# One layer of a conformer trunk on one core: the head's load order, unread matmuls in the stands, shares between VectorE and GpSimd, and a joint last group

## The chip, the cores and the metric

The kernel runs on one core of a Trainium2 chip. The metric is device time in microseconds (us), the median of several executions; lower is better. TensorE (PE) multiplies, with a weight load (PEld) ahead of each matmul; VectorE (DVE), ScalarE (ACT) and GpSimd (POOL) do the elementwise work; SyncE (SP) issues the DMAs.

## What is computed

All in fp32, for 1024 tokens of width D = 1024. With `DEPTH = 1` only the first mixer, the convolution module, is run, and only the latent tokens:

```python
mod_l = (silu(c) @ w_mod + b_mod)                       # 6 vectors of 1024
sh1, s1, g1, sh2, s2, g2 = split(mod_l, 6)
h = rms_norm(x, norm1_g) * (1 + s1) + sh1
u = h @ w_pw1 + b_pw1;  a, gate = split(u, 2)
u = dwconv(a * sigmoid(gate), w_dw) + b_dw              # 31 taps, inside segments of 64 tokens
u = silu(layer_norm(u, ln_g, ln_b))
x = x + g1 * (u @ w_pw2 + b_pw2)
h = rms_norm(x, norm2_g) * (1 + s2) + sh2
x = x + g2 * (square(relu(h @ w1)) @ w2)                # hidden width 4096
return rms_norm(x, final_g)
```

## The kernel before

Channels lie on the 128 partitions in 8 chunks, tokens on the free axis, in two blocks of 512: A (b = 0) and B (b = 1). Each fp32 operand of a product is split into a high and a low part (`fp32r`): ACT casts the high part, DVE or POOL subtracts it for the low one (`split_lo`, `weights`, `first_weights`, `split_wide`; all of these subtractions have line L373). A product is three matmuls of 512 columns (L424 to L426, in the second half of the MLP L890 to L892).

The stages, in order:

- **Head** (L1008 to L1028). Loads by SP: the conditioning vector `craw` first, then block A's 8 tiles of x, then the modulation rows and first weights, chunk by chunk. ACT squares x (L488), DVE sums the squares, PE makes the mean in a "turned" form (tokens on partitions, L451), ACT the root (L506), DVE its reciprocal, PE spreads it again (L521), ACT copies it (L526). `mod_chunk` makes 128 entries of one modulation vector from 512 KB of `w_mod`: on DVE in one instruction (L568) or on POOL (L576) with two instructions on ACT behind it (L581, L584). `modulated` (L534, L549, L553) makes the operand, and PE runs 8 accumulations of 24 matmuls.
- **Conv A beside the first pointwise product of B.** PE does ten pairs of `PW1_ORDER`, 48 matmuls each. Of the 31 taps of a chunk three start the sums, `POOL_TAPS` go to POOL (L703, after a multiply on ACT, L698), `PE_TAPS` to PE as diagonal matrices in plain fp32 (L668), and the others to DVE (L713). L723 and L732 add the sums up.
- **Layer norm A** (`layer_norm`: L747 subtracts the mean, L488 squares, L446 feeds the mean on PE, L499 root, L501 reciprocal, L759 multiplies, L764 silu).
- **Second pointwise product A** (`pointwise2`, 8 outputs of 24 matmuls; L779 adds to x), with the rows of `G1`, `S2`, `SH2` made chunk by chunk; then `norm2` A, with the two pairs of `PW1_LATE` behind it on PE.
- **First MLP product of A** (`up_first`, 32 outputs n of 24 matmuls, results to DRAM), beside conv B, whose chunk c has the turn `CONV_B[c]` = 3c in units of n. At n = `LN_B` = `PW2_B` = 22 come layer norm B, the second pointwise product B and `norm2` B.
- **8 groups of the second MLP product.** Seven groups (`mlp_joint`) do both blocks with seven instead of eight block products, at the price of eight sums and differences (`plus`, engines `S_ENG`, `T_ENG`) and of splits of the seven pairs (`WLO_ENG`, `HLO_ENG`); a wave is one product of 24 matmuls. Between the first waves PE does four outputs of B's first product for the next group. After wave `GATE` the next group's loads may start. The last group (`mlp_apart`) does four waves for A, then four for B, and `finish` norms and stores each block.

Every instruction's place is set by hand-written planning at build time (`Plan`): each operation has an engine, a cost and a turn, and at each moment an engine takes the ready operation of the lowest turn, if it has a buffer (`SLOTS`, `CAPS`; an operation over `NEAR` turns ahead must leave `KEEP` buffers free). `SYNC` is the delay that the plan assumes between engines. A POOL instruction and a DVE instruction that reads SBUF alone (`port`) are planned one after the other, never together. The result is a fixed order on each engine and on SP's queue; each engine runs in order and waits on semaphores.

## Time and profile before

| | us |
|---|---|
| median of 3 runs | 1033.12 (1032.26 to 1034.19) |
| the profiled execution, time | 1034.25 |
| its span in the trace | 1032.4 |

| engine | busy, share of the span |
|---|---|
| PE matmul | 95% |
| PE weight load | 76% |
| DVE | 67% |
| POOL | 58% |
| ACT | 51% |

TensorE's granted clock is 0.986 of full speed in the mean. The 16 DMA engines move 125 MB, 121 GB/s over the span; only the first 55 us are filled by transfers (362 and 404 GB/s in the first two of 40 slices). A busy PE is not PE at its peak, since the ends of pipelined matmuls are modelled; the count of matmuls in a stretch says more. The chain that ended last goes almost all over PE's matmuls of the MLP.

### The profile page before, as it was taken

Reading aid. Unit: us, or ns where it says so; the run is one execution under the profiler, and the core shown is the slowest. Engines: PE = TensorE matmul, PEld = TensorE weight load, DVE = VectorE, ACT = ScalarE, POOL = GpSimd, SP = SyncE. Lnnn points to the kernel's source line nnn. Section 1 sums busy time; section 2 is a strip of 40 time slices with the busy share of each in tenths; the row PEclk is TensorE's granted clock in tenths of the full one; section 3 lists DMA queues with packets and bytes.
Section 4 is the critical chain, followed back from the end, with each engine's and each line's share of the span. In section 5 each row is a group of like instructions: output and inputs, shape, how many; then the busy total and the mean of one; then the engine's idle time right before and its main releaser. Section 6 shows DMA issues by size and latency. Waiting matters only on the chain. (4 is left out here: it accounts for less than half of the span.)

```text
span 1032.4 us, 11676 instructions
## 1 busy us (share of the span) xinstructions
PE 977.8 (95%) x4182; PEld 786.8 (76%) x4182; DVE 687.4 (67%) x941; ACT 524.0 (51%) x767; POOL 597.9 (58%) x366
## 2 busy tenths in 40 slices
PE   2999999959899999999999999999999999999994
PEld 1877767638688888788887888888788788878873
DVE  6979999996399991523265475665658565575453
ACT  5469566795667775763264434243252424342123
POOL 0049799989948999661347346437263462732324
PEclk9999999989999999999999999999999999999996
DMA  9920223445446444554151501504023040303012
GB/s 362 404 79 1 82 82 135 172 163 184 160 123 219 139 146 153 176 173 161 41 204 41 183 21 45 180 1 168 37 73 131 21 163 21 123 1 123 1 63 101
DMA packets 52522, 125.27 MB, mean 121 GB/s; under 512 B 4464, under 2 KB 21104, under 8 KB 52464
## 3 DMA queue, kind: packets, MB, share of 16 engines
q1 hardware_dynamic: 52464, 124.53, 34.3%
q8 instruction: 33, 0.54, 0.2%
q14 instruction: 25, 0.20, 0.1%
HBM read 111.93 MB, written 12.58 MB: 121 GB/s over the span
## 5 line engine op out<-in xcount | busy, mean ns | idle before, releaser
L373 POOL TENSOR_TENSOR big<-big 128x1024 fp32r<-128x1024 f32 (+1 forms) x144 | 351.0, 2454 | 303.3 <-DVE big L373 139.6
L424 PE MATMUL bank<-big 128*128 128x512 f32 x896 | 355.1, 396 | 10.8 <-ACT big L366 8.6
L426 PE MATMUL bank<-big 128*128 128x512 f32 x896 | 351.1, 392 | 1.7 <-POOL small L628 1.2
L425 PE MATMUL bank<-big 128*128 128x512 f32 x896 | 351.1, 392 | 0.8 <-DVE big L373 0.5
L779 DVE SCALAR_TENSOR_TENSOR small<-bank,mod,small 128x512 f32<-128x512 f32 x228 | 167.4, 747 | 215.3 <-PE bank L892 171.9
L424 PEld LDWEIGHTS bank<-big 128*128 128x128 f32 x896 | 169.5, 189 | 50.6 <-ACT big L366 9.4
L713 DVE SCALAR_TENSOR_TENSOR bank<-small,vec,bank 128x432 f32<-128x432 f32 (+10 forms) x323 | 200.9, 694 | 2.4 <-ACT bank L650 1.5
L425 PEld LDWEIGHTS bank<-big 128*128 128x128 f32 x896 | 169.3, 189 | 40.2 <-issue 2.1
L426 PEld LDWEIGHTS bank<-big 128*128 128x128 f32 x896 | 169.2, 189 | 37.9 <-POOL small L628 1.9
L891 PE MATMUL bank<-big 128*128 128x512 f32 x456 | 178.1, 391 | 3.4 <-POOL big L373 3.4
L890 PE MATMUL bank<-big 128*128 128x512 f32 x456 | 178.0, 390 | 0.0
L373 DVE TENSOR_TENSOR big<-big 128x1024 fp32r<-128x1024 f32 (+2 forms) x126 | 159.5, 1285 | 27.4 <-ACT big L386 12.5
L892 PE MATMUL bank<-big 128*128 128x512 f32 x456 | 177.5, 389 | 0.0
L850 ACT CAST big<-big 128x1024 fp32r<-128x1024 f32 x106 | 108.1, 1048 | 121.4 <-POOL big L373 52.8
L703 POOL TENSOR_TENSOR small<-small 128x392 f32<-128x392 f32 (+4 forms) x108 | 113.5, 1084 | 13.9 <-ACT small L698 9.7
L373 POOL TENSOR_TENSOR small<-small 128x512 f32<-128x512 f32 x46 | 59.7, 1301 | 93.6 <-ACT small L488 64.9
L386 ACT CAST big<-big 128x1024 fp32r<-128x1024 f32 x92 | 95.1, 1040 | 25.6 <-POOL big L373 25.2
L891 PEld LDWEIGHTS bank<-big 128*128 128x128 f32 x456 | 85.6, 188 | 23.6 <-POOL big L373 5.7
L890 PEld LDWEIGHTS bank<-big 128*128 128x128 f32 x456 | 85.6, 188 | 18.5 <-DVE small L976 0.4
L892 PEld LDWEIGHTS bank<-big 128*128 128x128 f32 x456 | 85.6, 188 | 17.6
L488 ACT ACTIVATE small<-small 128x512 f32<-128x512 f32 x64 | 38.4, 627 | 81.3 <-DVE small L779 78.3
L838 ACT ACTIVATE small<-bank 128x512 f32<-128x512 f32 x32 | 19.2, 599 | 110.0 <-PE bank L426 110.0
(65 smaller groups left out, 627.6 us busy)
## 6 DMA issues: line engine op xcount, KB each, us to landing
big<-in_w SPq DMA_DIRECT2D x96, 512.0 KB, 3.8
big<-in_wmod SPq DMA_DIRECT2D x48, 512.0 KB, 5.3
big<-in_wpw SPq DMA_DIRECT2D x28, 512.0 KB, 4.6
hidden<-small SPq DMA_DIRECT2D x32, 256.0 KB, 2.4
big<-hidden SPq DMA_DIRECT2D x16, 512.0 KB, 5.9
small<-in_xA SPq DMA_DIRECT2D x16, 256.0 KB, 4.1
big<-in_wfirst SPq DMA_DIRECT2D x8, 512.0 KB, 10.2
small<-in_xB SPq DMA_DIRECT2D x16, 256.0 KB, 6.0
```

What stands on the lines that cost most here:

```text
L373: lambda: eng_of[o.eng].tensor_tensor(out=out(), in0=a(), in1=b(), op=op), r, w, part=part, port=port,
L386: plan.op("act", c_act(D), lambda: act.copy(t(wh), t(raw)), [raw], [wh], also=[wl])
L424: pe.matmul(o, wh, hi(a)[:, s], start=first, stop=False)
L425: pe.matmul(o, wh, lo(a)[:, s], start=False, stop=False)
L426: pe.matmul(o, wl, hi(a)[:, s], start=False, stop=last)
L703: return pool.tensor_tensor(out=dst, in0=dst, in1=seg(t(m))[:, :, tt], op=ALU.add)
L713: dve.scalar_tensor_tensor(out=dst, in0=src, scalar=w, in1=dst, op0=ALU.mult, op1=ALU.add)
L779: lambda s=s, p=p: dve.scalar_tensor_tensor(out=t(x)[:, s], in0=cut(s, p), scalar=scale.t, in1=t(x)[:, s], op0=ALU.mult, op1=ALU.add,),
L850: plan.op("act", c_act(D), lambda: act.copy(t(h), t(x)), [x], [h], also=[l])
L890: pe.matmul(t(p), t(wh)[:, cs], t(hh)[:, ns], start=first and k == 0, stop=False, skip_group_check=not first)
L891: pe.matmul(t(p), t(wh)[:, cs], t(hl)[:, ns], start=False, stop=False, skip_group_check=not first)
L892: pe.matmul(t(p), t(wl)[:, cs], t(hh)[:, ns], start=False, stop=k == 1, skip_group_check=not first)
```

## The change

- Head: block A's x is loaded ahead of `craw`; the load of the sqrt table hangs on the last square instead of on `csil`; the first chunk reads the reciprocal root from PSUM, not from ACT's copy.
- `warm`: 8, 4, 6 and 11 matmuls of 128 columns on constants, whose result nothing reads: behind x's fourth tile, the head's root, the head's reciprocal root and layer norm A's reciprocal root.
- Of the 24 modulation chunks for `G1`, `S2` and `SH2`, all on POOL before, 12 go to DVE (3, 1 and 8). The loads of `G2` wait for conv A and then one for each output of `up_first`.
- The 32 low parts of `up_first`'s weights go from POOL to DVE (`UP_LO`).
- Taps: on PE 25 to 28 for A and 0 to 2 for B, on POOL 46 to 47 for A and 62 as before for B. `PW1_ORDER` has another order; `LN_B` and `PW2_B` go from 22 to 21.
- Groups: two of the four sums on POOL instead of one, other engines for the splits (POOL's number stays 7 of 14), `GATE` 3 to 2.
- The last group is joint: seven waves, no outputs of B's first product between them; A's outputs are complete at the fifth wave, B's at the seventh. Its sums of squares: A all added on DVE with one feed, B five added on POOL and three fed directly. Both blocks' last root is not turned; 3 of 8 last multiplies of each block go to POOL (before: of B alone).
- Layer norm B feeds its last two squares directly; `norm2` B's root is not turned.
- The plan's own numbers: `SYNC` by engine, other costs, `KEEP`, `NEAR`, `CAPS`. These may move any instruction.

```diff
-POOL_TAPS = ((5, 8, 5, 10, 5, 4, 7, 2), (10, 7, 5, 7, 8, 7, 9, 9))
+POOL_TAPS = ((7, 8, 6, 9, 5, 5, 4, 3), (10, 9, 8, 7, 10, 6, 7, 5))
-    (0, 4), (0, 5), (1, 0), (1, 1), (0, 6),
-    (0, 7), (1, 4), (1, 5), (1, 6), (1, 7),
+    (0, 4), (0, 5), (1, 0), (1, 4), (1, 5),
+    (0, 6), (0, 7), (1, 6), (1, 7), (1, 1),
-LN_B, PW2_B = 22, 22
-PE_TAPS = ((4, 2, 4, 4, 2, 2, 2, 5), (0, 0, 0, 0, 0, 0, 0, 0))
+LN_B, PW2_B = 21, 21
+PE_TAPS = ((2, 6, 2, 2, 2, 2, 5, 7), (0, 0, 2, 0, 0, 0, 0, 0))
-UP_LO = ("pool", "pool")
-S_ENG, T_ENG = ("dve", "dve", "pool", "dve"), ("dve", "dve", "dve", "dve")
-GATE = 3
-WLO_ENG, HLO_ENG = ("pool", "pool", "dve", "pool", "dve", "dve", "pool"), ("dve", "pool", "dve", "pool", "dve", "pool", "dve")
+UP_LO = ("dve", "pool")
+S_ENG, T_ENG = ("pool", "pool", "dve", "dve"), ("dve", "dve", "dve", "dve")
+GATE = 2
+WLO_ENG, HLO_ENG = ("dve", "pool", "dve", "dve", "dve", "pool", "pool"), ("dve", "pool", "dve", "dve", "pool", "pool", "pool")
-HEAD_DIRECT, LNA, LNB, N2B, FA = 0, 8, 0, 0, 1
-TURNED = (True, False, False, False, True, True)
+HEAD_DIRECT, LNA, LNB, N2B, FA = 0, 8, 2, 0, 0
+TURNED = (True, False, False, False, False, False)
-FIN_POOL = 3
-S2_ENG, G1_ENG = ("pool",) * 8, ("pool",) * 8
+WARM = (8, 4, 6, 11)
+LAST_JOINT = True
+FA_ENG, FB, FB_ENG = "dve", 3, "pool"
+FIN_POOL = (3, 3)
+S2_ENG, G1_ENG = ("pool", "pool", "dve", "pool", "pool", "pool", "pool", "pool"), ("pool", "pool", "pool", "dve", "dve", "pool", "dve", "pool")
+SH2_ENG, G2_ENG = ("dve", "dve", "dve", "dve", "dve", "dve", "dve", "dve"), "dve"
-KEEP = {"big": 2, "small": 3}
-NEAR = 2.0
-CAPS = {"raw": 4, "head": 7, "w": 8, "tmp": 6, "tap": 4, "taps": 4, "acc": 8, "wave": 14}
+KEEP = {"big": 4, "small": 2}
+NEAR = 120.0
+CAPS = {"raw": 4, "head": 7, "w": 10, "tmp": 4, "tap": 3, "taps": 4, "acc": 8, "wave": 12}
-    SYNC = 70
+    SYNC = {"pe": 200, "act": 140, "dve": 130, "pool": 80, "dma": 70}
...
+    def warm(n, after):
+        if not n:
+            return
+        p = new("bank", [P, BANK])
+        def emit():
+            for i in range(n):
+                pe.matmul(t(p)[:, :P], ones.t, ones.t, start=True, stop=True)
+        plan.op("pe", n * 220, emit, [ones, after], [p])
...
+        if b == 0:
+            warm(WARM[3], rstd)
...
-        run(s1, t1, q, True, (1, 1))
-        run(s4, b22, q, False, (1, 0))
-        run(a12, b21, r, True, (0, 0))
+        if g + 1 < NQ:
+            run(s1, t1, q, True, (1, 1))
+            run(s4, b22, q, False, (1, 0))
+            run(a12, b21, r, True, (0, 0))
+        else:
+            close(0, 1)
+            run(a12, b21, r, True, (0, 0))
+            close(0, 0)
+            run(s1, t1, q, True, (1, 1))
+            close(1, 1)
+            run(s4, b22, q, False, (1, 0))
+            close(1, 0)
+            finish(0, xls[0], sums[0])
+            finish(1, xls[1], sums[1])
...
+    xs0 = load_x(0)
     craw = new("big", [P, D], F32, "raw")
     plan.op("dma", 1460, lambda: sp.dma_start(t(craw), cvec.partition_broadcast(P)), w=[craw], lag=2000)
-    xs0 = load_x(0)
...
+    warm(WARM[0], xs0[3])
     for k in range(KC):
-        add_square(ms, xs0[k])
+        sq = add_square(ms, xs0[k])
     plan.op("act", c_act(D), lambda: act.activation(csil.t, t(craw), AF.Silu), [craw], [csil], "silu")
-    preload(AF.Sqrt, "sqrt", csil)
-    r0 = rstd_of(ms, False)
+    preload(AF.Sqrt, "sqrt", sq)
+    r0, r0_bank = rstd_of(ms, False, WARM[1])
+    warm(WARM[2], r0)
...
-        mod_chunk(S2, j, S2_ENG[j])
-        mod_chunk(SH2, j, S2_ENG[j])
+        mod_chunk(S2, j, S2_ENG[j], gate=conv_end(S2_GATE, j))
+        mod_chunk(SH2, j, SH2_ENG[j], gate=conv_end(S2_GATE, j))
...
-            mod_chunk(G2, n)
+            mod_chunk(G2, n, G2_ENG, gate=[up_op] if n else conv_end(7, 0))
...
-    sums = Mean(0, FA), Mean(1, 1, turned=TURNED[5])
+    sums = Mean(0, FA, FA_ENG), Mean(1, FB, FB_ENG, turned=TURNED[5])
...
-        if g + 1 < NQ:
-            mlp_joint(g, 2200 + 100 * g, lambda n: n < 5 and up_part(g + 1, n - 1))
+        if g + 1 < NQ or LAST_JOINT:
+            mlp_joint(g, 2200 + 100 * g, lambda n: n < 5 and g + 1 < NQ and up_part(g + 1, n - 1))
```

## Rows read from the trace of the kernel before

**Rows 1.** The page, parts 1 and 2: busy times; PE in 40 slices

```profile
PE 977.8 (95%) x4182; PEld 786.8 (76%) x4182; DVE 687.4 (67%) x941; ACT 524.0 (51%) x767; POOL 597.9 (58%) x366
PE   2999999959899999999999999999999999999994
```

**Rows 2.** Windows: length, busy PE PEld DVE ACT POOL (instructions), clock, DMA, GB/s

```profile
20.00:30.00 10.00, 7.83 (x25) 5.97 (x26) 9.64 (x17) 4.28 (x8) 0.00 (x0) 1.00 1.03 410
...
250.00:260.00 10.00, 10.00 (x46) 8.29 (x45) 1.62 (x4) 4.88 (x9) 10.00 (x7) 1.00 0.46 157
...
270.00:280.00 10.00, 7.23 (x21) 4.81 (x21) 3.77 (x3) 6.92 (x10) 10.00 (x5) 0.83 0.50 159
280.00:300.00 20.00, 20.00 (x89) 16.55 (x89) 18.52 (x28) 12.93 (x18) 10.93 (x8) 1.00 0.42 131
300.00:400.00 100.00, 100.00 (x443) 82.80 (x442) 86.68 (x141) 72.95 (x114) 92.40 (x66) 1.00 0.47 159
```

**Rows 3.** Timeline of the head: start, us, instruction [idle before <-releaser]

```profile
7.15 1.28 ACT L994 ACT_TABLE_LOAD   x1
...
8.45 0.29 ACT L994 ACTIVATE sc<-csil,eps 128x1 f32<-128x1 f32 x1
...
9.29 4.68 DVE L373 TENSOR_TENSOR small<-small 128x512 f32<-128x512 f32 x6 [1.44 <-ACT small L488]
...
13.89 1.28 DVE L568 CUSTOM_DVE_ANT_0 big<-big,csil,vec 128x1024 f32<-128x1024 f32 x1
...
17.59 2.04 PE L521 MATMUL bank<-small,ones 128*128 128x512 f32 x2 [1.70 <-DVE small L512]
...
21.85 0.80 PE L424 MATMUL bank<-big 128*128 128x512 f32 x1 [2.22 <-ACT big L549]
```

**Rows 4.** Timeline of layer norm A

```profile
217.17 3.35 DVE L501 RECIPROCAL bank<-bank 128x512 f32<-128x512 f32 x1
...
220.24 1.04 ACT L581 ACTIVATE big<-big 128x1024 f32<-128x1024 f32 x1
...
221.39 1.28 ACT L764 ACT_TABLE_LOAD   x1
...
224.21 0.79 PE L424 MATMUL bank<-big 128*128 128x512 f32 x1 [8.57 <-ACT big L366]
```

**Rows 5.** Timelines of DVE and ACT at the second norm of A

```profile
270.78 0.75 DVE L779 SCALAR_TENSOR_TENSOR small<-bank,mod,small 128x512 f32<-128x512 f32 x1 [0.37 <-PE bank L426]
...
272.26 1.06 ACT L581 ACTIVATE big<-big 128x1024 f32<-128x1024 f32 x1 [2.08 <-POOL big L576]
...
273.64 0.61 ACT L488 ACTIVATE small<-small 128x512 f32<-128x512 f32 x1
```

**Rows 6.** Groups by form: instructions, count | busy us, mean ns | idle before

```profile
L373 DVE TENSOR_TENSOR big<-big 128x1024 fp32r<-128x1024 f32 x61 | 81.0, 1333 | 15.1 <-ACT big L386 12.5 <-ACT big L850 1.6 <-issue 0.6
...
L713 DVE SCALAR_TENSOR_TENSOR bank<-small,vec,bank 128x448 f32<-128x448 f32 x32 | 20.7, 683 | 0.1
...
L373 POOL TENSOR_TENSOR big<-big 128x1024 fp32r<-128x1024 f32 x137 | 333.5, 2450 | 294.1 <-DVE big L373 130.4 <-DVE small L373 61.6 <-ACT big L850 48.6
...
L446 PE MATMUL bank<-small,ones 128*128 128x512 f32 x38 | 18.0, 603 | 7.1 <-ACT small L488 4.6 <-ACT small L612 1.7 <-POOL small L373 0.8
...
L668 PE MATMUL bank<-small,diag 128*128 128x408 f32 x12 | 5.0, 513 | 0.2 <-ACT diag L661 0.2
```

**Rows 7.** Waits of DVE from 290 to 430: waiter <- awaited, us, times, longest

```profile
DVE small L732 <- POOL small L703: 19.8, 4, 12.3
```

**Rows 8.** Waits of PE over the whole span

```profile
PE bank L891 <- POOL big L373: 3.4, 4, 1.6
```

**Rows 9.** Timelines of PE and POOL at the end

```profile
1012.92 0.39 PE L892 MATMUL bank<-big 128*128 128x512 f32 x1
1016.33 3.54 PE L451 MATMUL bank<-ones,small 128*128 128x1 f32 x16 [3.02 <-POOL small L373]
...
1023.99 3.71 POOL L373 TENSOR_TENSOR small<-small 128x512 f32<-128x512 f32 x3 [7.72 <-ACT small L968]
```

More of the change, by code (lines that the diff above doesn't have):

```diff
@@ L215, in run @@
                         a.left -= 1
-                        a.ready = max(a.ready, o.end + (0 if a.eng == o.eng else self.SYNC))
+                        a.ready = max(a.ready, o.end + (0 if a.eng == o.eng else self.SYNC[o.eng]))
                         if not a.left:
@@ L305, in c_pool, with load @@
     def c_pool(n):
-        return 80 + 2.15 * n
+        return 150 + 2.14 * n
     def c_tt(eng, n):
         return {"dve": c_dve(n), "pool": c_pool(n), "any": {"dve": c_dve(n), "pool": c_pool(n)}}[eng]
-    def load(buf, src, n, after=()):
+    def load(buf, src, n, after=(), gate=()):
         plan.op(
-            "dma", n * P * 4 / 360, lambda: sp.dma_start(t(buf)[:, :n], src), after, [buf], lag=2000
+            "dma", n * P * 4 / 360, lambda: sp.dma_start(t(buf)[:, :n], src), after, [buf], lag=2000,
+            gate=gate,
         )
@@ L456, in feed @@
             if self.turned:
-                plan.op("pe", 350 * QT, emit_turned, [x, ones], banks(self.acc))
+                plan.op("pe", 450 * QT, emit_turned, [x, ones], banks(self.acc))
             else:
@@ L490, in add_square, with rstd_of @@
         mean.add(sq)
-    def rstd_of(mean, in_bank=True):
+        return sq
+    def rstd_of(mean, in_bank=True, hot=0):
         ((_, p),) = mean.acc
@@ L501, in rstd_of @@
             plan.op("dve", 6.4 * TB[mean.b], lambda: dve.reciprocal(t(r), t(r)), [r], [r])
-            return r
+            return r if in_bank else (r, r)
         root = Buf(None, None, const.tile([P, QT], F32, name="root"))
@@ L507, in rstd_of @@
         )
+        warm(hot, root)
         plan.op("dve", 100, lambda: dve.reciprocal(root.t, root.t), [root], [root])
@@ L526, in rstd_of @@
         plan.op("act", c_act(TB[mean.b]), lambda: act.copy(t(r), t(p)), [p], [r])
-        return r
+        return r, p
+    def warm(n, after):
[6 more added lines that the diff above has]
+        plan.op("pe", n * 220, emit, [ones, after], [p])
     def modulated(b, x, rstd, scale, shift, in_place, eng="dve"):
@@ L559, in modulated, with mod_chunk @@
         return out
-    def mod_chunk(v, i, eng="dve", cap="raw"):
+    def mod_chunk(v, i, eng="dve", cap="raw", gate=()):
         raw = new("big", [P, D], F32, cap)
-        load(raw, wmod[v * KC + i], D)
+        load(raw, wmod[v * KC + i], D, (), gate)
         m, bias = mod[v][i], col(C_MOD, v * KC + i)
@@ L791, in pointwise2 @@
         plan.op(
-            "pool", 140 + 0.85 * TB[b],
+            "pool", 235 + 0.85 * TB[b],
             lambda: pool.tensor_scalar(t(x), t(x), 1.0, g1b[j].t, op0=ALU.mult, op1=ALU.add),
@@ L822, in up_first @@
         plan.op("act", c_act(TB[0]), lambda: act.activation(t(r), t(p), AF.Relu), [p], [r])
-        plan.op("act", c_act(TB[0]), lambda: act.activation(t(r), t(r), AF.Square), [r], [r])
+        o = plan.op("act", c_act(TB[0]), lambda: act.activation(t(r), t(r), AF.Square), [r], [r])
         to = hidden[n // 2]
@@ L828, in up_first @@
         )
+        return o
     def wide():
@@ L933, in run, with close @@
             step(n)
+        def close(b, o):
+            for j in range(4):
+                add_square(sums[b], xls[b][4 * o + j])
         run(a11, b11, z, True, (0, 0))
@@ L958, in finish @@
     def finish(b, xl, ms):
-        n = FIN_POOL if b else 0
+        n = FIN_POOL[b]
         for j in range(KC - n, KC):
@@ L993, in preload @@
             "act", 200,
-            lambda: act.activation(sc1t[:, 0:1], after.t[:, 0:1], func, bias=eps.t[:, 0:1], scale=0.0),
+            lambda: act.activation(sc1t[:, 0:1], (after.t if after.t is not None else t(after))[:, 0:1], func, bias=eps.t[:, 0:1], scale=0.0),
             [after, eps], [sc1[0]], table,
@@ L1026, in trunk @@
         scale_column(sc1[k], mod[S1][k], C_N1, k)
-        h1[0].append(modulated(0, xs0[k], r0, sc1[k], mod[SH1][k], True))
+        h1[0].append(modulated(0, xs0[k], r0 if k else r0_bank, sc1[k], mod[SH1][k], True))
         for u in range(2 * NF):
@@ L1070, in trunk, with conv_end @@
     vA = layer_norm(0, LNA)
+    def conv_end(c, j):
+        return () if c is None else list(cv[0, min(c + j, KC - 1)].writers)
     xlA, msA = [], Mean(0, 1, turned=TURNED[2])
@@ L1073, in trunk @@
         plan.at(1400 + j)
-        mod_chunk(G1, j, G1_ENG[j])
+        mod_chunk(G1, j, G1_ENG[j], gate=conv_end(G1_GATE, j))
         plan.op(
@@ L1109, in trunk @@
             h2B = norm2(1, xls[1], msB)
-        up_first(n, h2A)
+        up_op = up_first(n, h2A)
     second = {}
```

2 lines of the change are left out of this document (1 added, 1 removed).

## The prediction

> **What bounds the kernel now.** I read the busy times first, then the slices, the windows, the timelines at each dip of PE, and the waits. PE is busy 95% of the span and near full in all but three places: the head, the slices around layer norm A and norm 2 of A, and the end [rows 1]. In a full stretch 443 matmuls start in 100 us, 0.226 us each [rows 2]; a wave of 24 is 5.4 us. So the kernel is bound by the number of matmuls, plus the stands of PE, and an edit on another engine counts only where PE stands or is made to stand. The work beside PE has two places without room. DVE runs at 96% in the head, and in 300 to 400 us DVE has 86.7 and POOL 92.4 us of work in 100 [rows 2].
>
> The profiled execution took 1034.25 us, 1.85 more than its span, and 1.13 more than the median of 1033.12. I sum against 1034.25 and take 1.13 off at the end. A measurement can tell about 0.2% (2 us) from no change.
>
> **The last group and the end: -7.5.** Joint instead of apart takes 24 of 192 matmuls away: 24 x 0.226 = -5.4. A's mean needs one feed instead of two; a feed is two fp32 matmuls, 38 of which take 18.0 us [rows 6], so -0.9. Against it, the joint group needs eight sums and six more low parts, and its waves follow each other without the four products that stand between the waves of the other groups. Some waves there already waited for POOL, 1.6 us at the longest [rows 8]. I put +1.5 here, between 0 and 5.5 (a whole wave late).
>
> The tail: the last matmul starts at 1012.92, is through at 1013.15, and the span ends 19.3 later. POOL's three last multiplies end at 1027.7 [rows 9], so the stores take 4.7 more. Until then PE's turned feeds wait 3.0 for POOL's queue of adds and take 3.5 [rows 9]. After the change three squares are fed directly, and the chain from the last matmul is 0.2 + 0.75 (the add to x) + 0.6 (square) [rows 5], 0.95 (feed), about 0.9 (root and its waits), 3.35 (full reciprocal, [rows 4]), 0.6 (copy), 3.7 (POOL), 4.7 (stores) and some 0.8 of waits between: 16.6. That is -2.7. Bounds 0 (DVE also has five multiplies of A in its way, 3.7) and -4. Sum -5.4 - 0.9 + 1.5 - 2.7 = -7.5.
>
> **The head: -3.2.** A table load (1.28) and its dummy activation (0.29) stand among the squares now, and DVE's adds end at 9.29 + 4.68 = 13.97 [rows 3]. With x first and the table behind, the squares end 1.3 (512 KB of `craw` at 410 GB/s, [rows 2]) to 2.6 us earlier. But `csil` now comes after that table load. By the plan's costs the last square ends at about 8.4 and `craw` lands at 9.3, so the plan puts the sqrt load first (these two numbers say the order only). `csil` is a silu, so its table must be loaded again, and the root then needs sqrt once more: two loads more, 2.6. From squares that end near 10.0: 10.0 + 1.6 + 1.3 + 1.05 (a 1024-wide activation, [rows 4]) = 13.9, just where the first `mod_chunk` on DVE starts now (13.89). DVE therefore starts no earlier. The gain lies behind it: the copy to SBUF is gone for the first chunk (about 0.7), the spreading matmul took 2.04 at half pace where a feed takes 0.95 (-1.1), and in 20 to 30 us only 25 matmuls started where 8.15 us (from 21.85) have room for 36, 2.5 lost to slow pace and waits [rows 2, 3]. The unread matmuls should save 1.4 of these. Sum -3.2. DVE works 96% of the time there [rows 2] and its start does not move, so if a chunk takes it longer than PE's 5.4, the gain ends with DVE. On SP's queue nothing behind `craw` changes its place. Bounds: 0 (this, or the reloads) and -5.
>
> [...]
>
> **Conv A: +1.5.** PE gets three taps more, two matmuls each at 0.42 [rows 6], +2.5, all on its path. DVE has 4 taps less (0.68 each, -2.7), POOL one more. DVE and PE end this stage together, so I take +1.5. Bounds -1.5 and +5: the second if modulation chunks (1.36 each on DVE) are put between taps.
>
> **Layer norm A: -2.0.** After the reciprocal PE waits until 224.21, 8.6 us idle [rows 4]. 1.3 of these are the silu table, loaded at 221.39 only because ACT still had chunk sums (L581, 220.24) to do [rows 4]; half of these leave ACT. Behind the stand PE ran at half pace, and the 11 unread matmuls are to end that sooner. But if they start at half pace themselves, 22 short matmuls stand in front of the real ones. A 512-column pair takes 0.95, so these take 11 x 0.24 = 2.6 at full and 5.2 at half pace, against a stand of 3.7 from the reciprocal's end. So +1.5 at worst, -3.7 at best (table and pace).
>
> **Norm 2 of A: -3.3.** The last add ends at 271.5, and its square starts at 273.64, behind a chunk sum that waited 2.1 for POOL's multiply [rows 5]. In 270 to 280 only 21 matmuls start instead of 44, at a mean granted clock of 0.83, 5.2 us lost [rows 2]. With 12 of 24 chunks moved, POOL (full in 250 to 260 while DVE has 1.6 of 10 us, [rows 2]) is through earlier. What is left is add, square and waits, 1.9. So -3.3, between -4.5 and 0.
>
> **Conv B and `up_first`: +5.** DVE gets 32 low parts of 1.333 us, where POOL had 2.450 [rows 6]. This is the dangerous edit. From 280 to 400 DVE has 105.2 us of work [rows 2], and its idle time is above all one wait of 12.3 for POOL's last taps [rows 7]. PE starts on its products behind norm 2 at about 274.9; until output 21 it has 96 + 504 matmuls, 135.6 us, so it wants the 22nd weights at 410.5. DVE must by then have done the 21 earlier ones, 28.0 us: 280 + 105.2 + 28.0 = 413.2, and 1.4 for the last sums. What belongs to conv B has a lower turn than the 22nd weights, so DVE does it first and PE waits, about 4. Later ends are hidden: 11 outputs, 60 us, cover layer norm B. Each gated load of `G2` waits for the output that SP's store just ahead of it waits for too, so nothing new is held up on SP. The two taps cost 1.7, two more feeds 1.9, less 1 for the mean that is no longer turned, and 1.6 of PE's waits in this stage go. Sum +5; bounds 0 and +10.
>
> **Group starts: -2.** Four waits of PE for POOL, 3.4 together [rows 8]. Loads start one wave earlier, and the first wave no longer needs POOL, but the second has four POOL operations in line (two sums, two low parts, 9.8 us) as before. Here I also put what the new plan numbers may shift anywhere: each misplaced instruction costs what these do, about 1. Bounds -3.4 and +5.
>
> Sum: -7.5 - 3.2 + 1.5 - 2.0 - 3.3 + 5 - 2 = -11.5. 1034.25 - 11.5 - 1.13 = **1021.6**.
>
> **Rivals.**
> - *DVE becomes the bound in conv B* (slower). The first two chunks of conv B are now done before 250, in DVE's gaps of layer norm A; the 12 moved modulation chunks (12 x 1.36 = 16.3 us) have the lower turn and take these gaps. DVE's free time in 250 to 280 (8.4 us in 10, [rows 2]) can hold them, if buffers allow. If not, conv B ends 16.3 later and PE waits 20 instead of 4: 1037.9. It is slower than now from a wait of about 17.5 on. Against it: that free time is there.
> - *The stands close and DVE keeps up* (better). Conv B starts early in the freed gaps and PE never waits for weights (-5), all group waits go (-1.4), layer norm A gives 3.5 (-1.5): 1013.7.
> - *Head and last group give little.* The reloads eat the head (+3.2) and the joint group starves for a wave (+4): 1028.8. [...]
> - *The change does not act*: unread matmuls miss the stands, waits come back elsewhere: about 1033.
>
> **How the numbers follow.** Forecast 50% (1016 to 1027), better 17%, head and last group 19%, DVE bound 11%, no effect 3%. The range leaves out the slower case and the best end: 1012 to 1031. Faster by over 0.2%: 50 + 17 + 17 (a little of the third case lies at 1031) = 84%; within: 5%; slower: 11%.
>
> **What would show it.** Last group: 168 matmuls, and a tail of some 16.6 us behind the last. Head: four table loads ahead of the first product, which starts near 20. Norm 2: no dip of the clock in 270 to 280. Conv B: no 12 us wait of DVE for POOL, DVE over 95% until about 410, and a PE wait for DVE's low parts (L373) at output 21. I am wrong if PE waits over 10 us in conv B, if layer norm A's first product starts later behind the reciprocal than 3.7 us by more than 2, or if the joint group has waits of over 5 us.

## The result and the profile after

| | before | after |
|---|---|---|
| median, us | 1033.41 (1032.26 to 1034.19, 4 runs) | 1022.56 (1021.19 to 1023.30, 4 runs) |
| ratio | | 0.9894, 95% interval 0.9877 to 0.9911 |
| span of the profiled execution, us | 1032.44 | 1020.55 |

The forecast was 1021.6. The sum is nearly exact and several of its terms are not: layer norm A is 9.8 us worse than forecast, conv A 4.8 and conv B 5.6 better. That the sum comes out is luck.

To see where time went, I follow one count through both traces: the start of the n-th matmul of a product (from 0; up to the last group the n-th is the same place in the work). The shift is after minus before.

| stage, read off at | before, us | after, us | shift | of this stage | forecast |
|---|---|---|---|---|---|
| head (n = 24) | 29.98 | 28.93 | -1.05 | -1.05 | -3.2 |
| conv A (end of the feeds of its mean on PE) | 206.69 | 202.36 | -4.33 | -3.28 | +1.5 |
| layer norm A, second pointwise product (n = 863, last ahead of norm 2) | 270.28 | 273.79 | +3.51 | +7.84 | -2.0 |
| norm 2 A (n = 864) | 274.87 | 274.47 | -0.40 | -3.91 | -3.3 |
| conv B, `up_first`, layer norm B (n = 2100) | 564.70 | 563.75 | -0.95 | -0.55 | +5 |
| seven groups (n = 3684) | 926.74 | 922.79 | -3.95 | -3.00 | -2 |
| last group, end of span | 1032.44 | 1020.55 | -11.89 | -7.94 | -7.5 |

Names and lines of the kernel after: products L429 to L431 (second MLP product L912 to L914), unread matmuls L544, feeds L451 and L456, spread L528, modulation on DVE L587 and on POOL L595, taps on DVE L732 and on POOL L722, low parts L378, layer norm's subtraction L766, reciprocal L507, multiply L780.

The page, parts 1 and 2, as in [rows 1]:

```profile
PE 980.4 (96%) x4210; PEld 791.7 (78%) x4210; DVE 757.2 (74%) x1008; ACT 520.1 (51%) x748; POOL 513.8 (50%) x328
PE   5999999959999999999999999999999999999994
```

84 us of work left POOL and 70 came to DVE. Of PE's three dips, the one at layer norm A stayed.

Windows of after, columns as in [rows 2]:

```profile
20.00:30.00 10.00, 9.22 (x42) 7.59 (x41) 9.05 (x16) 5.14 (x9) 0.00 (x0) 0.92 1.02 408
200.00:210.00 10.00, 3.70 (x8) 1.58 (x7) 9.96 (x20) 4.46 (x8) 4.70 (x3) 0.80 0.04 17
...
220.00:240.00 20.00, 12.84 (x45) 9.87 (x44) 19.36 (x31) 17.61 (x30) 9.40 (x10) 0.74 0.43 161
...
270.00:280.00 10.00, 10.00 (x42) 7.61 (x41) 5.93 (x5) 6.50 (x11) 8.68 (x5) 1.00 0.30 107
...
300.00:400.00 100.00, 100.00 (x443) 82.77 (x442) 99.26 (x149) 72.48 (x114) 52.27 (x50) 1.00 0.48 167
```

Three rows answer to [rows 2]: 42 matmuls instead of 25 in 20 to 30, of which 12 are unread ones and 29 (before 25) are of products; 42 instead of 21 in 270 to 280, at a granted clock of 1.00; and 443 in 300 to 400 as before, though DVE is full there. In 200 to 210 PE is busy for 3.7 us while DVE is full: that is the stage to look at.

Timeline of after's head [rows 3]:

```profile
1.05 3.71 PE L544 MATMUL bank<-ones 128*128 128x128 f32 x16 [1.05 <-DVE eps L1025]
...
10.76 1.28 ACT L1031 ACT_TABLE_LOAD   x1
12.05 0.29 ACT L1031 ACTIVATE sc<-small,eps 128x1 f32<-128x1 f32 x1
...
12.37 1.28 ACT L1054 ACT_TABLE_LOAD   x1
...
14.73 1.28 ACT L512 ACT_TABLE_LOAD   x1
...
14.75 1.28 DVE L587 CUSTOM_DVE_ANT_0 big<-big,csil,vec 128x1024 f32<-128x1024 f32 x1 [2.67 <-ACT csil L1054]
...
18.21 2.04 PE L528 MATMUL bank<-small,ones 128*128 128x512 f32 x2 [2.30 <-ACT big L410]
20.05 2.26 PE L544 MATMUL bank<-ones 128*128 128x128 f32 x12
...
20.91 0.75 DVE L553 SCALAR_TENSOR_TENSOR small<-small,sc,bank 128x512 f32<-128x512 f32 x1 [1.52 <-ACT small L533]
...
22.47 0.49 PE L429 MATMUL bank<-big 128*128 128x512 f32 x1 [0.16 <-ACT big L568]
```

The reloads came as forecast (with one at 0.73, four in all). `csil` ends at 14.72 and DVE's first chunk starts at 14.75, 0.86 later than before. The first unread matmuls run at 1.05 and end 7.4 us ahead of PE's next matmul (12.13), and the spreading matmul still takes 2.04. The read straight from PSUM (L553) starts at 20.91, behind ACT's copy (20.29 to 20.88), all the same; why was not tried. The first product starts at 22.47, 0.62 later than before. What was won is the pace behind it: the products follow 0.226 apart from 23.9 on.

Timeline of after's layer norm A [rows 4]:

```profile
195.88 0.75 DVE L742 SCALAR_TENSOR_TENSOR small<-bank,vec,small 128x512 f32<-128x512 f32 x1
...
205.93 1.28 DVE L732 SCALAR_TENSOR_TENSOR bank<-small,vec,bank 128x448 f32<-128x448 f32 x2
207.12 4.87 DVE L766 TENSOR_TENSOR small<-small,bank 128x512 f32<-128x512 f32 x8
...
208.66 9.15 PE L451 MATMUL bank<-small,ones 128*128 128x512 f32 x16 [6.30 <-ACT small L493]
...
217.65 2.62 PE L544 MATMUL bank<-ones 128*128 128x128 f32 x22
...
218.55 3.37 DVE L507 RECIPROCAL bank<-bank 128x512 f32<-128x512 f32 x1 [0.85 <-ACT bank L505]
...
224.19 0.80 PE L429 MATMUL bank<-big 128*128 128x512 f32 x1 [3.92 <-ACT big L371]
...
227.48 2.50 DVE L378 TENSOR_TENSOR big<-small,big 128x512 fp32r<-128x512 f32 x4
...
228.23 0.79 PE L430 MATMUL bank<-big 128*128 128x512 f32 x1 [3.24 <-DVE big L378]
```

and of before, lines that [rows 4] does not have:

```profile
201.22 0.75 DVE L723 SCALAR_TENSOR_TENSOR small<-bank,vec,small 128x512 f32<-128x512 f32 x1
...
207.11 4.86 DVE L747 TENSOR_TENSOR small<-small,bank 128x512 f32<-128x512 f32 x8
...
208.50 7.13 PE L446 MATMUL bank<-small,ones 128*128 128x512 f32 x16 [1.81 <-ACT small L488]
...
225.49 0.80 PE L425 MATMUL bank<-big 128*128 128x512 f32 x1 [0.49 <-DVE big L373]
```

After the change the mean of conv A had left PE at 202.4; the subtractions start at 207.12, behind modulation chunks and block B's taps in DVE's order. The unread matmuls run ahead of the reciprocal, not behind it. The first product starts when it did before (224.21); the second comes 4.0 after the first, before 1.3.

Norm 2 A [rows 5]: the last add, and its square 0.03 behind it:

```profile
274.29 0.75 DVE L800 SCALAR_TENSOR_TENSOR small<-bank,mod,small 128x512 f32<-128x512 f32 x1 [3.09 <-PE bank L431]
...
275.07 0.63 ACT L493 ACTIVATE small<-small 128x512 f32<-128x512 f32 x1 [3.18 <-DVE small L800]
```

End of conv B, timelines of DVE and PE:

```profile
409.75 1.41 DVE L751 TENSOR_TENSOR small<-bank,small 128x512 f32<-128x512 f32 x2
411.07 4.62 DVE L378 TENSOR_TENSOR big<-big 128x1024 fp32r<-128x1024 f32 x4
...
413.37 1.88 PE L451 MATMUL bank<-small,ones 128*128 128x512 f32 x4
414.68 0.80 PE L429 MATMUL bank<-big 128*128 128x512 f32 x1
```

The first of the four low parts belongs to output 21, whose first product (n = 1464) starts at 414.68. The waits there, of DVE for POOL from 290 to 430 [rows 7] (19.8 before), then all of PE's from 290 to 570:

```profile
DVE small L751 <- POOL small L722: 0.4, 2, 0.2
```

```profile
PE bank L451 <- POOL small L378: 0.7, 1, 0.7
```

The end [rows 9]:

```profile
1002.49 0.39 PE L914 MATMUL bank<-big 128*128 128x512 f32 x1
...
1004.16 2.84 PE L451 MATMUL bank<-small,ones 128*128 128x512 f32 x6 [0.42 <-ACT small L493]
...
1007.96 3.36 DVE L507 RECIPROCAL bank<-bank 128x512 f32<-128x512 f32 x1
...
1012.80 3.71 POOL L378 TENSOR_TENSOR small<-small 128x512 f32<-128x512 f32 x3 [5.50 <-ACT small L1005]
```

### The profile page after: what moved, and what is told of

Read it like the earlier page. It is cut to its first block, busy times and chain, and to the rows that moved or that the text cites. A ratio compares the mean times of both kernels' runs of the same rounds, so it can differ in the third digit from the quotient of the medians.

```text
span 1020.5 us, 11766 instructions
## 1 busy us (share of the span) xinstructions
PE 980.4 (96%) x4210; PEld 791.7 (78%) x4210; DVE 757.2 (74%) x1008; ACT 520.1 (51%) x748; POOL 513.8 (50%) x328
## 4 chain that ended last, share of the span: by engine, by line
PE 75%; DVE 19%; POOL 2%; issue 2%; ACT 1%; DMA 1%; SPq 0%; POOLq 0%; DVEq 0%; ACTq 0%
PE bank L430 14%; PE bank L431 14%; PE bank L429 14%; DVE bank L732 12%; PE bank L913 10%; PE bank L914 10%; PE bank L912 10%; PE bank L451 2%; DVE big L378 1%; POOL small L378 1%; DVE bank L507 1%; DVE small L751 1%; POOL small L722 1%; DVE big L587 1%; DVE small L640 1%
## 5 line engine op out<-in xcount | busy, mean ns | idle before, releaser
L378 POOL TENSOR_TENSOR big<-big 128x1024 fp32r<-128x1024 f32 (+1 forms) x124 | 299.0, 2421 | 339.0 <-DVE big L378 155.6
L429 PE MATMUL bank<-big 128*128 128x512 f32 x896 | 355.0, 396 | 4.1 <-ACT big L371 3.9
L431 PE MATMUL bank<-big 128*128 128x512 f32 x896 | 349.7, 390 | 0.0
L800 DVE SCALAR_TENSOR_TENSOR small<-bank,mod,small 128x512 f32<-128x512 f32 x240 | 176.6, 748 | 197.1 <-PE bank L914 158.3
L378 DVE TENSOR_TENSOR big<-big 128x1024 fp32r<-128x1024 f32 (+2 forms) x160 | 198.6, 1262 | 27.4 <-POOL big L378 9.7
L872 ACT CAST big<-big 128x1024 fp32r<-128x1024 f32 x112 | 113.4, 1050 | 193.8 <-POOL big L378 60.0
L732 DVE SCALAR_TENSOR_TENSOR bank<-small,vec,bank 128x464 f32<-128x464 f32 (+11 forms) x318 | 200.5, 697 | 1.7
L429 PEld LDWEIGHTS bank<-big 128*128 128x128 f32 x896 | 168.9, 188 | 41.8 <-ACT big L371 4.1
L431 PEld LDWEIGHTS bank<-big 128*128 128x128 f32 x896 | 168.8, 188 | 35.2
L912 PE MATMUL bank<-big 128*128 128x512 f32 x448 | 174.7, 390 | 0.0
L914 PE MATMUL bank<-big 128*128 128x512 f32 x448 | 174.3, 389 | 0.0
L722 POOL TENSOR_TENSOR small<-small 128x400 f32<-128x400 f32 (+4 forms) x109 | 113.3, 1067 | 50.4 <-DVE big L378 27.8
L391 ACT CAST big<-big 128x1024 fp32r<-128x1024 f32 x92 | 95.6, 1043 | 23.4 <-POOL big L378 11.0
L912 PEld LDWEIGHTS bank<-big 128*128 128x128 f32 x448 | 84.1, 188 | 17.7 <-issue 0.2
L914 PEld LDWEIGHTS bank<-big 128*128 128x128 f32 x448 | 84.1, 188 | 17.4
L378 POOL TENSOR_TENSOR small<-small 128x512 f32<-128x512 f32 x39 | 52.1, 1340 | 83.3 <-DVE big L378 44.3
L717 ACT ACTIVATE small<-small,vec 128x400 f32<-128x400 f32 (+4 forms) x109 | 62.9, 629 | 0.0
```

What stands on the lines that cost most here:

```text
L378: lambda: eng_of[o.eng].tensor_tensor(out=out(), in0=a(), in1=b(), op=op), r, w, part=part, port=port,
L391: plan.op("act", c_act(D), lambda: act.copy(t(wh), t(raw)), [raw], [wh], also=[wl])
L429: pe.matmul(o, wh, hi(a)[:, s], start=first, stop=False)
L431: pe.matmul(o, wl, hi(a)[:, s], start=False, stop=last)
L722: return pool.tensor_tensor(out=dst, in0=dst, in1=seg(t(m))[:, :, tt], op=ALU.add)
L732: dve.scalar_tensor_tensor(out=dst, in0=src, scalar=w, in1=dst, op0=ALU.mult, op1=ALU.add)
```

## The experiments

Shifts are against the profile of after, at the same n. Kernels with after's head show n = 24 up to 1.4 earlier than that profile did (0.2, 0.6, 0.6, 0.7, 0.85, 0.95 and 1.4 in seven of them), so a head's shift within this says little. In the same seven DVE's first chunk starts at 13.26 to 14.23, around the 13.89 of before; only the profile of after has it at 14.75. The intervals of the ratios of e1, e2, e3, e6, e7, e8 and e9 overlap with that of after; e4, e5, e10, e11 and e12 are clear of it. What the first seven say rests on the places in one profile each.

**e1_no_warm: no unread matmuls.**

```diff
-            for i in range(n):
+            for i in range(0):
                 pe.matmul(t(p)[:, :P], ones.t, ones.t, start=True, stop=True)
```

> The changed kernel without its 29 unread matmuls, all else in the same order. Theory A: nothing on the chip holds them back until the thing they were planned behind, since they do not read it. In the changed kernel 8 of them run at 1 us, and the 11 of layer norm A run at 217.7 us, right behind the feeds and before the reciprocal; by its first product PE stands again and is at half pace. So without them layer norm A is as before: first product 224 us, half pace to 233; only the 6 that end next to the head's first product did something, and the time rises by 1 to 2 us (1023.5 to 1024.5). Rival: they keep the clock up as meant; then both stands get slower, 3 to 5 us more (1026 to 1028).

1024.65 us, ratio 0.9913 (0.9890 to 0.9936). Shifts: +1.37 at n = 24, +1.97 behind layer norm A, no more afterwards. By this profile all 29 of them together are worth 2 us, most of it in the head; norm 2 A's gain does not come from them (n = 864 follows n = 863 by 0.68, as in after).

**e2_filled: as many as fill the stands.**

```diff
-WARM = (8, 4, 6, 11)
+WARM = (8, 4, 6, 11); FILL = {8: 37, 4: 20, 6: 9, 11: 27}
-            for i in range(n):
+            for i in range(FILL[n]):
```

> The changed kernel with more unread matmuls at the same four places (37, 20, 9 and 27 instead of 8, 4, 6 and 11), so many that they reach from where they can start to the end of the stand; all else in the same order. Theory A: the clock is then up at the head's spreading matmul (0.86 us instead of 2.04) and at layer norm A's first products (0.23 us apart from the start instead of 0.43 until 233); 3 to 4 us less (1018.5 to 1019.5). Rival: the pace there is set by ScalarE's and VectorE's feed, and the clock is beside the point: 0 to 1 us less (1021.5 to 1022.5).

1021.15 us, ratio 0.9882 (0.9865 to 0.9898); -1.62 at n = 24, -1.73 at n = 700 and at the end. The shift in the head is little more than the scatter named above; what is sure is the spreading matmul, which takes 1.10 instead of 2.04. The time lies between the two expectations, because layer norm A gave nothing more. PE's timeline there:

```profile
215.95 6.19 PE L544 MATMUL bank<-ones 128*128 128x128 f32 x54
222.49 0.50 PE L429 MATMUL bank<-big 128*128 128x512 f32 x1 [0.35 <-ACT big L371]
226.52 0.80 PE L430 MATMUL bank<-big 128*128 128x512 f32 x1 [3.53 <-DVE big L378]
```

The first product takes 0.50 us (0.80 in after). Then PE stands 3.5 for the first low part, and ten products run 0.43 apart, just as many as in after.

**e3_csil_first: the sqrt load behind `csil`, as it was.**

```diff
-    preload(AF.Sqrt, "sqrt", sq)
+    preload(AF.Sqrt, "sqrt", csil)
```

> The sqrt table load hangs on csil again instead of on the last square, so that the silu of the conditioning vector needs no second load of its table. Theory B: the reload holds up VectorE's first modulation chunk (14.75 us in the changed kernel, 13.89 in the one before); it now starts at about 12.7 us, and the head's products run 1.5 to 2 us earlier than in the changed kernel. The total gains less, 0 to 2 us (1020.5 to 1022.5), as layer norm A's start is held by other work on VectorE. Rival: the head is bound by the landings and by the root's chain: the first product stays within 0.5 us and the total within 1.

1019.92 us, ratio 0.9871 (0.9853 to 0.9888). DVE's first chunk starts at 13.29, waiting for its data and no longer for `csil`; -1.14 at n = 24. Both lie within the scatter (e6, with the reload, has 13.26 and -1.44), so a gain in the head is not shown, and the time is 0.6 below the expected range. The edit also makes another plan: the subtractions of layer norm A start at 204.62, the first low part at 224.25, behind six of the eight multiplies, and the shift is -3.47 at n = 700, of which half is lost again by n = 2100.

**e4_apart: the last group as it was.**

```diff
-LAST_JOINT = True
+LAST_JOINT = False
```

> The last group apart, eight waves instead of seven, its end as in the changed kernel (roots not turned, three direct feeds). Theory C: the joint group is worth its whole wave: 5.4 us, and as much again as its prompt end for A takes from the tail: 5 to 7 us more (1027.5 to 1029.5). Rival: the joint group's waves wait for splits and give back half: 2 to 3 us more (1024.5 to 1025.5).

1029.08 us, ratio 0.9958 (0.9944 to 0.9971). The shift is -0.66 at n = 3684 and +7.39 at the end of the span: the joint group is worth 8.0 there, 5.4 of it the 24 matmuls of a wave. But 3.4 are a stand that this run has at the start of its last group and before has not: the wait of 1.8 below, and 1.6 in the products behind it.

```profile
PE bank L913 <- DVE big L378: 1.8, 1, 1.8
```

Without the stand the joint group is worth some 4.6 here.

**e5_ln_first: modulation chunks and block B's taps held behind layer norm A's subtractions.** `first_ln` is the list of these subtractions.

```diff
-                [raw, csil, vec], [raw, m], port=True,
+                [raw, csil, vec], [raw, m], port=True, gate=first_ln,
...
-                plan.op("dve", c_stt(reach(s, k)), fma, [u, vec, p], [p])
+                plan.op("dve", c_stt(reach(s, k)), fma, [u, vec, p], [p], gate=first_ln if b else ())
```

> In the planner's order the modulation rows' VectorE chunks and block B's convolution taps on VectorE are kept behind layer norm A's five subtractions; the rest of the order is planned anew around that. After the change the subtractions began at 207.12 although the mean feed had left TensorE at 202.4, with modulation chunks and taps of block B ahead of them in VectorE's order. Theory D (that work is what ate layer norm A's gain): the subtractions begin near 202.5 to 203.5, the first product behind layer norm A comes near 220 (224.19 after the change), and of the 4 us some 3 to 4 last to the end: 1018.5 to 1020. Rival (layer norm A is bound by its own chain of VectorE and ScalarE steps behind the subtractions, or the work held back comes due before norm 2): the first product no earlier than 223 or the gain given back by the first product behind norm 2 (N = 864): 1021.5 to 1024.

1029.50 us, ratio 0.9952 (0.9934 to 0.9970). The theory's place and the rival's loss both came true, and the time lies outside of both ranges. The subtractions start at 201.48; the shift is -6.77 at the first product behind layer norm A and -8.30 at n = 700. Then it turns to +5.70 at n = 863. Its windows, and PE's longest wait after 240:

```profile
185.00:205.00 20.00, 18.42 (x73) 13.30 (x72) 15.00 (x25) 5.96 (x10) 0.00 (x0) 1.00 0.00 0
```

```profile
271.61 1.80 PE L451 MATMUL bank<-small,ones 128*128 128x512 f32 x2 [3.92 <-POOL small L378]
```

No transfer ran from 185 to 205: at most four raw tiles may be held (`CAPS`), and modulation rows that wait for their chunk hold them. The rows for the second pointwise product were then made until 276, and PE waited for them. That the raw tiles are the cause is read from this window, not tried by itself.

**e6_mods_pool: all 24 chunks on POOL again.**

```diff
-S2_ENG, G1_ENG = ("pool", "pool", "dve", "pool", ...), ("pool", "pool", "pool", "dve", ...)
-SH2_ENG, G2_ENG = ("dve", ...), "dve"
+S2_ENG, G1_ENG = ("pool",) * 8, ("pool",) * 8
+SH2_ENG, G2_ENG = ("pool",) * 8, "dve"
```

> The modulation rows are all on GpSimd again as before the change; all else stays the change's. Theory (the rows shared out are what lets norm 2 A's square stand right behind its add, and their price is VectorE's time ahead of layer norm A): layer norm A's subtractions begin 3 to 5 us earlier than 207.12, and norm 2 A's stand of 3 to 4 us comes back, with the first product behind norm 2 no earlier than after the change: total 1021.5 to 1025. Rival 1 (the norm 2 gain has another cause, the order of the square): the stand stays away and layer norm A gains: 1018 to 1020. Rival 2 (GpSimd becomes late for its taps in convolution B, VectorE waits again): 1026 to 1032.

1023.81 us, ratio 0.9896 (0.9879 to 0.9912): no difference from after. Norm 2's stand does not come back (n = 864 at 273.83, 0.23 behind n = 863):

```profile
274.88 0.63 ACT L493 ACTIVATE small<-small 128x512 f32<-128x512 f32 x1 [3.87 <-DVE small L800]
```

And layer norm A does not gain: with fewer chunks on DVE, block B's taps fill its order, and the subtractions start near 206. So sharing the rows out is neither the cause of norm 2's gain nor the price at layer norm A.

**e7_edge: ten more of conv B's taps on DVE.**

```diff
-POOL_TAPS = (..., (10, 9, 8, 7, 10, 6, 7, 5))
+POOL_TAPS = (..., (10, 9, 8, 5, 8, 4, 5, 3))
```

> Ten more of convolution B's taps stand on VectorE in place of GpSimd. Theory (VectorE has about 1 us to spare by the end of convolution B: its weight splits for output 21 ended at 412.2 and TensorE wanted them at 413.3): ten taps of 1.2 to 1.33 us are 12 to 13 us more, so TensorE waits some 8 to 12 us for VectorE between 400 and 440, and the total is 1030 to 1035. Rival (there is slack that the order hides, splits that can be planned ahead of taps): less than 3 us: 1022 to 1025.5.

1023.07 us, ratio 0.9888 (0.9873 to 0.9903). From n = 960 to n = 2100 1.6 us are lost, not 8 to 12. I had priced the taps wrongly: 318 taps (L732) take DVE 200.5 us in after, 0.63 each, so ten are 6.3. PE's waits from 290 to 570:

```profile
PE bank L451 <- DVE small L751: 1.4, 1, 1.4
PE bank L431 <- DVE big L378: 0.6, 1, 0.6
```

Of 6.3 us more on a DVE that is full, PE sees 2.5 at n = 1464 and 1.6 at n = 2100: there were some 4 us of slack, which a share of 99% does not show.

**e8_up_half: every second low part of `up_first` on POOL.**

```diff
-        p = mlp_up(0, n, h2, UP_LO[0])
+        p = mlp_up(0, n, h2, "pool" if n % 2 else "dve")
```

> Every second low part of the first up-projection's weights is made on GpSimd (2.45 us each) in place of VectorE (1.33 us): VectorE has some 13 us less to do between 300 and 410. Theory (VectorE is full there but no product waits for it): the products' milestones from N = 960 to N = 2100 stay within 1 us of the change's, total 1021.5 to 1023.5. Rival (the prediction's term: VectorE's fullness costs some 4 to 5 us in this stage): 1017.5 to 1019. Other rival (GpSimd's low parts at 2.45 us come too late for TensorE): 1024 to 1028.

1021.58 us, ratio 0.9873 (0.9858 to 0.9887). From n = 960 to n = 1440 nothing moves; 0.95 is won by n = 1536, at layer norm B. DVE's window shows the room that it got:

```profile
400.00:412.00 12.00, 12.00 (x54) 9.95 (x53) 4.63 (x5) 4.34 (x6) 4.68 (x2) 1.00 0.47 158
```

DVE is busy for 4.63 of these 12 us, in after for 11.96, and PE does its 54 matmuls either way. DVE's fullness costs PE about 1 us, not 5.

**e9_ln_taps: only block B's taps held behind the subtractions** (the second edit of e5 alone).

> Only block B's convolution taps on VectorE are kept behind layer norm A's subtractions in the planner's order; the modulation chunks may still go ahead of them. Holding back both gave a first product behind layer norm A 6.8 us earlier, and 12 us of new waits before norm 2. Theory (the taps may wait without harm; the modulation chunks held back kept their buffers full and so the later loads away): five modulation chunks of 1.3 stand between the last sums near 197.3 and the subtractions, which begin near 204.5 instead of 207.12; the first product behind layer norm A comes near 221.5 and this stays to the first product behind norm 2: 1019 to 1020.5. Rival (taps held back are themselves what comes late before norm 2): waits of TensorE between 240 and 275 as before them, 1022 or more.

1020.29 us, ratio 0.9873 (0.9858 to 0.9889).

```profile
202.86 4.86 DVE L767 TENSOR_TENSOR small<-small,bank 128x512 f32<-128x512 f32 x8
```

The subtractions start 4.26 earlier than in after. The first product comes at 223.34, only 0.85 earlier, and as much (0.84) is there at n = 24 already: the chain up to the first product won nothing. ACT's own order holds its squares back, behind three operations for block B (L670):

```profile
205.86 2.17 ACT L493 ACTIVATE small<-small 128x512 f32<-128x512 f32 x4
```

PE stood until 206.53, and its 16 matmuls for the squares then took 10.1 us (9.2 in after, 7.1 in before). The shift is -2.65 at n = 700 and -2.24 at the end. The 1.8 between n = 672 and n = 700 come from the first low part, which has no tap ahead of it (225.70 for 227.48), and from six products instead of ten at 0.43. So the time is as expected, by another way. Part of layer norm A's loss is the order of DVE's filling work, the start of the subtractions alone does not bring it back, and taps may wait where modulation rows may not. Unread matmuls between the mean's feeds and the squares' were not tried.

**e10_three: e2, e3 and e8 together.**

> Three edits together: the sqrt table's load behind csil, the unread matmuls as many as fill their stands (37, 20, 9, 27), and every second low part of the first up-projection on GpSimd. Alone they gave, by their profiles' milestones, 1.7, 1.7 and 1 us. If they add up (theory: they act at different places, the fill mostly in the head, the other order mostly in layer norm A): 1018 to 1019.5. If the head's two gains are the same gain (both end with VectorE's first modulation chunk): 1019.5 to 1021.

1016.24 us, ratio 0.9831 (0.9813 to 0.9849), the fastest of all and below the expected ranges. By the ratios the three alone add up to 5.8 us and this run gives 6.5, the same within the noise. Shifts: -1.95 at n = 24, -5.15 at n = 700, -6.08 at n = 2100. Its timeline at layer norm A:

```profile
203.88 4.87 DVE L766 TENSOR_TENSOR small<-small,bank 128x512 f32<-128x512 f32 x8
...
223.07 0.68 DVE L378 TENSOR_TENSOR big<-small,big 128x512 fp32r<-128x512 f32 x1
```

```profile
222.14 0.50 PE L429 MATMUL bank<-big 128*128 128x512 f32 x1 [0.77 <-ACT big L371]
223.81 0.50 PE L430 MATMUL bank<-big 128*128 128x512 f32 x1 [1.17 <-DVE big L378]
```

Here the plan puts no tap ahead of the subtractions, and the first low part ahead of the last two multiplies, as in e3. Between n = 24 and n = 700 it gives 3.2, e3 2.3 and e2 0.1: the filling, worth nothing there in e2, seems to give 0.9 where the stand behind the first product is short. This rests on one profile; e11, with the same filling, gives 2.4 there.

**e11_woven: as e10 (with every third low part on POOL), and the last three multiplies of layer norm A behind the first three low parts.**

```diff
-                [x, rstd], [x], port=rstd.size != "bank",
+                [x, rstd], [x], port=rstd.size != "bank", gate=los[c - 5 : c - 4] if c > 4 else (),
```

> As the three together (with every third low part on GpSimd), and in layer norm A the multiplies of the sixth to eighth chunk stand behind the low parts of the first to third in VectorE's order. After the change the first low part came at 227.48, behind all eight multiplies, and TensorE waited 3.2 us for it after its first product. Theory (that stand is one of order alone, and it sends TensorE back to half pace): the second product follows within 1.5 us of the first, products stand at 0.226 us within 5 us of it, and the gain over the three alone is 1.5 to 3 us at N = 700: 1016 to 1018. Rival (the multiplies of the last chunks come late then, and TensorE waits for them): no gain over the three alone, 1018 to 1020.5.

1017.94 us, ratio 0.9847 (0.9831 to 0.9862); -3.98 at n = 700, 1.2 less than e10. The second product follows 1.33 after the first, as expected, but it takes 0.80 already, and the products are 0.43 apart until 229.5. e10's plan had the order of the low part anyway; forcing it gained nothing. Ahead of the first product PE stood 1.72 here and 0.77 in e10.

**e12_up_pool: all low parts of `up_first` on POOL.**

```diff
-UP_LO = ("dve", "pool")
-CAPS = {..., "w": 10, ..., "wave": 12}
+UP_LO = ("pool", "pool")
+CAPS = {..., "w": 8, ..., "wave": 14}
```

> The low parts of the first up-projection's weights are back on GpSimd, as before the change, with the two buffer limits of before for split weights (8) and waves (14); all else, the shared modulation rows too, is the change's. Two questions. Norm 2 A: with all rows on GpSimd the stand stayed away, so the rows are not its cause alone. Theory (either of two reliefs of GpSimd is enough, the rows shared out or block B's taps put later): no stand returns, the first product behind norm 2 follows the last one ahead of it within 1 us, as after the change (0.7). Rival (the up-projection's move is the cause): 3.5 us or more between them, as before the change (4.6). Conv B: with GpSimd at up to 2.45 us per low part again. Theory (GpSimd was the cause of VectorE's waits there, and TensorE was not waiting much either way): milestones from N = 960 to N = 2100 within 2 us of the change's, total 1021 to 1025. Rival (the move took waits of TensorE away): 3 us or more are lost there, 1026 to 1032.

1046.66 us, ratio 1.0136 (1.0117 to 1.0155): 24 us slower than after, at a place that neither expectation named. n = 671 comes 10.6 earlier and n = 672 23.0 later. PE has run its products ahead, and conv A's last two chunks stand in DVE's order behind nine modulation chunks (184 to 220). The last sum:

```profile
226.92 0.75 DVE L742 SCALAR_TENSOR_TENSOR small<-bank,vec,small 128x512 f32<-128x512 f32 x1
```

It stands at 195.88 in after. From n = 960 to n = 2100 it takes 0.54 less than after does, with this window:

```profile
300.00:400.00 100.00, 100.00 (x440) 82.28 (x439) 84.91 (x130) 69.35 (x106) 78.54 (x55) 1.00 0.46 152
```

This does not show that the move of the 32 low parts neither cost nor gave anything: while PE stood, DVE and POOL had got ahead (at n = 960 they had done 13 taps more than in after), and two buffer limits differ too. e8 answers it for half of the low parts. For norm 2 A the run answers nothing either, since all came 20 us later.

## Why the prediction was right or wrong

- **Last group and end: right** (-7.9 for -7.5), with two misses in it. The group is 6.5 shorter for 4.8: PE has no wait in it, where I put 1.5. The tail is 1.5 shorter for 2.7, 17.8 us for 16.6: three adds stood behind A's reciprocal on DVE (+1.2). e4 shows the gain and not its size.
- **Norm 2 A: right in place and size** (-3.9 for -3.3), not in its cause. I laid it to chunks taken off POOL; in e6 they are all on POOL and the gain stays. Nor is it only that PE came later: in e10 it comes earlier than in before (n = 863 at 268.63) and n = 864 follows by 0.69. In before, block B's taps stand among the rows on POOL between 204 and 220, and the last row starts at 269.8; in after and e6 few of these taps come so early, and the last row starts at 266.7 and 260.6. That this order is the cause was read from the traces and not tested alone.
- **Group starts: right** (-3.0 for -2). Three of the four waits of [rows 8], with the pace behind them, make 2.7 there in before, and after has none. The longest (1.65, at 560) lies ahead of n = 2100 and counts in the table's row above.
- **Head: right direction, a third of the size** (-1.05 for -3.2; up to -2.5 with the scatter between profiles). Of the three gains in my sum only the pace came (1.7 for 1.4). The direct read (0.7) gained nothing, as it started at 20.91, behind the copy (to 20.88); the spreading matmul (1.1) took 2.04 as before, as the first unread matmuls ran at 1.05. DVE's start, 0.9 later in this profile, is within the scatter of the 13.9 that I took. Behind the table load at 10.76, which ends at 12.04, an activation starts at 12.05.
- **Conv A: wrong, and for the better** (-3.3 for +1.5). The last sums stand at 195.88 to 197.35 and not near 202, 5 us earlier, though PE has more taps. Which of the edits did this was not tried.
- **Layer norm A: the step that failed** (+7.8 for -2.0). I took it that the subtractions start when conv A is through, since they did so before, 0.4 behind its mean. After the change DVE's order held four modulation chunks and seven block B operations ahead of them, so they start at 207.12 as before, 4.8 behind the mean: 4.3 lost. PE stood idle from 202.4 for 6.3 us and began the feeds of the squares at a granted clock of 0.50 (208.66 to 211), which puts the reciprocal 1.4 back [rows 4]. The silu table gave as much back: it is loaded at 220.85, and the first product comes 2.3 behind the reciprocal's end for 3.7. So the first product starts as before. The first low part stood behind eight multiplies and a tap, before behind seven multiplies; the second product comes at 228.23 for 225.49, and ten products instead of four run 0.43 apart. That makes 2.74 + 6 x 0.2 = 3.9, against a shift of 3.8 at n = 700. My sum had neither the late start nor this wait; its bound of +5 for conv A named such filling, in another place.
- What shows the cause is e5: with the filling work held back the subtractions start at 201.48, the feeds of the squares take 7.1 and the first product comes 6.2 earlier, the head's shift taken off. The plan of the other engines changes with it, and by e9 an earlier start on DVE alone is lost again on ACT and PE.
- **The unread matmuls: wrong in how they are held.** Nothing that they read is made by what they were planned behind, so they run as soon as PE comes to them (217.65, ahead of the reciprocal).
- **Conv B and `up_first`: wrong by 5.6** (-0.55 for +5). The wait of about 4 did not come at all, and both times behind it were wrong. DVE was through with conv B and 21 low parts at 411.07 for my 414.6, and output 21's low part was ready at about 412.3. PE wanted it at 414.68 for my 410.5: I counted 600 products at full pace, 135.6 us, and nothing between them. From n = 864 to n = 1464 PE took 140.2, with a feed of norm 2, the two taps and the feeds at 413.37 in between; in before it took 139.3 already, which could have been read from its trace. By e7 there were some 4 us of slack.

Of the signs, the joint group's 168 matmuls, the four table loads, norm 2 without a dip of the clock and the full DVE until 410 came; the first product near 20 and the wait at output 21 did not. Of the rivals, "DVE becomes the bound in conv B" is refuted by e7 and e8. "The stands close and DVE keeps up" was half true: DVE kept up, and e10 shows that the stands could be made shorter, at 1016.2. "Head and last group give little" holds for the head and fell for the last group.

## What to carry to other kernels

In a fixed order on each engine, look at what stands ahead of the first link of a critical chain, not only at when its inputs are there: work that fills an idle engine delays the chain if the chain comes free meanwhile. Look so at every engine that the chain passes: in e9 DVE was freed and ACT's filling work held the chain. Hold back what needs no buffers that others wait for (taps here) and not what does (modulation rows). In these runs unread matmuls kept the pace only where they reached the next real matmul (the spreading one took 1.10 us in e2, and 2.04 in after, 2.30 behind them), and where no further stand followed at once (behind e2's of 3.5, ten products were 0.43 apart). A busy share of 99% says nothing of slack: compare the time at which a result is ready with the time at which it is wanted, with all of the waiting engine's other work counted in.

## What the runs showed of the hardware

- TensorE's pace fell in layer norm A's stands and did not come back at once: in after, behind stands of 3.9 and 3.2, ten products were 0.43 us apart (granted clock 0.50 from 228 to 232.5) before 0.23 returned; in e2, behind one of 3.5, ten as well. In e10 the stands were 0.8 and 1.2, and seven were 0.43 apart.
- The granted clock of a row missed this in before's head: products stand 0.43 apart from 23.55 to 26.54, and the clock of 20 to 30 reads 1.00 [rows 2].
- An activation starts 0.01 to 0.02 us behind a table load, in all loads of the head that one follows directly.
- A low part of 128x1024 on DVE took 1333 ns in the mean before [rows 6] and 1265 after, when POOL's share of 300 to 400 us had fallen from 92 to 52%. The means are over 61 and 96 low parts of other stages, and what sets this was not tried.
